# A pad of 192 bytes ahead of the weights' pool, so that all wide matmul operands begin at one address modulo 512

## The chip, the cores and the metric

The kernel runs on one core of a Trainium2 chip. The metric is the device time of one execution in microseconds. The engines that the text speaks of are TensorE (PE, the matmuls; PEld is its weight load), VectorE (DVE), ScalarE (ACT) and GpSimd (POOL); the SyncE queue (SP) issues the DMAs. A profile is one execution recorded by the hardware profiler.

## The reference

One block of a hybrid model for 512 tokens of width 1024, all in float32. A wide input projection feeds a state-space branch (SSD) and an attention branch with three dilations; both are gated and merged, and a gated feed-forward part with a short convolution follows.

```python
h = rms_norm(x, norm1_g[l])
proj = h @ w_in[l]
z, xbc, dt_raw, q, k, v, g_ssd, g_attn = jnp.split(proj, IN_SPLITS, axis=-1)
y_ssd = ssd_branch(z, xbc, dt_raw, ...)
y_attn = attn_branch(q, k, v, q_norm_g[l], k_norm_g[l])
merged = (jax.nn.sigmoid(g_ssd) * (y_ssd @ w_ssd_proj[l])
          + jax.nn.sigmoid(g_attn) * (y_attn @ w_attn_proj[l]))
x = x + merged @ w_out[l]
h2 = rms_norm(x, norm2_g[l])
u = causal_dwconv(h2 @ w_up[l], ffn_conv_w[l], ffn_conv_b[l])
u_gate, u_val = jnp.split(u, 2, axis=-1)
x = x + (jax.nn.silu(u_gate) * u_val) @ w_down[l]
```

## The kernel before

**How a product is made.** Every large product is done in split precision. A float32 operand is held as two tiles of the type float32r: a rounded part (`hh`, `h2h`, `mh`, `acth`, `whi` and so on) and the rest (`hl`, `h2l`, `ml`, `actl`, `wlo`). A product is the sum of three matmuls: high with high, high with low, low with high. A matmul of the wide kind loads a block of 128 rows by 128 columns as weights (the stationary operand) and streams a block of 128 by 512 past it (the moving operand) into one PSUM bank of 512 float32 columns.

**Weights.** All weight matrices come in 194 pieces of 128 x 1024 elements, in a fixed order (`pieces`). `load_piece` has SP fetch a piece into a `raw` tile; `make_piece` lets ScalarE round it to `whi` (L99) and VectorE subtract to `wlo` (L100). `raw`, `whi` and `wlo` have three buffers each in the pool `weights`. `prefetch` and `next_piece` make pieces ahead of their use.

**Stages.** TensorE's order is written out by hand; the other engines follow a scheduler, with hand-written order in two places. The stages of wide matmuls, by PSUM tile: `ps_v` (L401) projects the tokens to the attention values; `ps_qk` (L477) to queries and keys; `ps_ssd` and `ps_gate` (`mm_chan`, L139) to the SSD channels and the gates; `ps_ap` (`mm_chan`, L139) is the attention's output projection; `ps_sp` (L918) that of SSD; `ps_wo` (L945) the projection of the merged branches; `ps_u` (`mm_chan`, L139) the up projection; `ps_wd` (L945) the down projection. In `ps_v`, `ps_wo` and `ps_wd` the activations are stationary and the weights move; in all others the weights are stationary. `mm_chan` runs 24 matmuls per bank (8 blocks of 128 channels times three products; 12 for `ps_ap`, which has 4 blocks). Small matmuls of the SSD and attention sides are put in between during the input projection. `ps_dt` (L309) is a narrow product of `hh` and `hl` with `wd2`, a tile of 64 columns per block.

**Where tiles lie.** Memory is 128 partitions wide; a tile takes the same bytes in each, and an address here means the byte in a partition. Pools are stacked from two ends. On the left stack, upward: `const` (`cp`), then `weights` (`wp`), then in turn `comb`, `hT` (`hh`, `hl`), `ssd_a`, later `merged` (`mh`, `ml`), `ysplit` (`yh`, `yl`), then `ffn` and `act` (`acth`, `actl`). On the right stack, downward from 229,344: `ssd_y` (`ysb`), `attn_out` (`ah`, `al`), `attn_a`, `attn_b`, `ssd_b`, `gates`, later `x1` (`x1`, `h2h`, `h2l`) and `norm2`. Tiles take multiples of 32 bytes. The pool `const` goes from 16,512 to 24,864; `weights` begins at 24,864, which is 48 x 512 + 288. All wide tiles are multiples of 512 bytes long.

| tiles | stack | first address | modulo 512 |
|---|---|---|---|
| `raw`, `whi`, `wlo` | left | 24,864 (raw), 37,152 (whi), 49,440 (wlo) | 288 |
| `hh`, `hl` | left | 72,480, 88,864 | 288 |
| `mh`, `ml` | left | 61,728, 78,112 | 288 |
| `yh`, `yl` | left | 94,496, 106,784 | 288 |
| `acth`, `actl` | left | 67,872, 112,928 | 288 |
| `ah`, `al` | right | 180,192, 188,384 | 480 |
| `h2h`, `h2l` | right | 196,576, 212,960 | 480 |
| `wd2` | left, in `const` | 22,432 | 416, and 160 for every second block |

Of the kernel before, what the change touches and what calls it, by code (L numbers as in the profile page):

```python
# [8 lines left out]
F32 = mybir.dt.float32  # L9
# [7 lines left out]
P = 128  # L17
# [21 lines left out]
def kernel(  # L39
# [14 lines left out]
    def pool(name, side="left", bufs=1):  # L54
        return tc.tile_pool(name=name, bufs=bufs, side=side, reuse_waits="tile")

    cp = ctx.enter_context(pool("const"))
# [118 lines left out]
    dtd = cp.tile([P, NT, 32], F32, tag="dtd", name="dtd")  # L176
    cdec = cp.tile([P, NT, 32], F32, tag="cdec", name="cdec")
    wd2 = cp.tile([P, KD, 64], F32R, tag="wd2", name="wd2")
    scr_a = dp.tile([32, S], F32, tag="scr_a", name="scr_a")
    scr_e = dp.tile([32, S], F32, tag="scr_e", name="scr_e")  # L180
    stat = dp.tile([S, 3, 16], F32, tag="stat", name="stat")
# [929 lines left out]
```

## Time and profile before

| | us |
|---|---|
| median of three runs | 1229.72 (1226.87 to 1229.96) |
| the profiled execution | 1228.72 |
| span of its trace, first to last instruction | 1227.0 |
| TensorE busy | 1217.5 |
| VectorE busy | 686.6 |
| ScalarE busy | 545.3 |

The mean granted clock of TensorE over the span is 0.997 of full speed. A busy time is the union of the records of an engine or a group. The records of successive matmuls overlap, because a matmul's record runs to the modelled end of its pipeline while the next one has already begun; the pace of TensorE is therefore read from the starts of its matmuls and not from the length of a record. The two slices of the profile's second part that show TensorE's clock and the DMA traffic:

```profile
PEclk9999989999999999999999999999999999999999
DMA  5445434322746444434235323342433333322330
```

Each digit is a fortieth of the span, in tenths: the clock is full nearly everywhere, and the DMA engines are busy a third to a half of the time.

### The profile page before, as it was taken

The numbers are of one execution on the slowest core, as the hardware profiler recorded it, in microseconds if no ns is written. First come the engines' busy times: TensorE is split into PE (matmuls) and PEld (weight loads), VectorE is DVE, ScalarE is ACT, GpSimd is POOL, SyncE is SP. The second block draws the span as 40 slices with busy tenths as digits, with TensorE's granted clock in tenths as the row PEclk, the third lists the DMA queues.
The fourth block names the chain that finished last, engine by engine and source line by source line (L and its number), as shares of the span: only waits on it lengthen the run. The fifth ranks groups of instructions, "written<-read, shape, count | busy, mean of one in ns | idle before, by whom it ended". The sixth has DMA issues, their size and how long they took to land.

```text
span 1227.0 us, 15111 instructions
## 1 busy us (share of the span) xinstructions
PE 1217.5 (99%) x5992; PEld 992.5 (81%) x5992; DVE 686.6 (56%) x908; ACT 545.3 (44%) x829; POOL 79.3 (6%) x57
## 2 busy tenths in 40 slices
PE   9999989999999999999999999999999999999998
PEld 7877767997888788888888888888888888888887
DVE  5233444447789986877645445555665565653322
ACT  4433555377746656455533424423544444341210
POOL 1011111100000102101111000000000000000000
PEclk9999989999999999999999999999999999999999
DMA  5445434322746444434235323342433333322330
GB/s 183 120 112 138 105 87 106 93 66 74 189 121 184 127 127 131 121 112 110 71 87 140 118 88 101 102 173 69 119 88 100 89 97 92 94 95 96 105 126 35
DMA packets 157625, 134.71 MB, mean 110 GB/s; under 512 B 12337, under 2 KB 125601, under 8 KB 156530
## 3 DMA queue, kind: packets, MB, share of 16 engines
q1 hardware_dynamic: 157553, 133.74, 37.8%
q8 instruction: 47, 0.77, 0.3%
q14 instruction: 25, 0.20, 0.1%
HBM read 131.12 MB, written 2.61 MB: 109 GB/s over the span
## 4 chain that ended last, share of the span: by engine, by line
PE 91%; DVE 3%; DMA 3%; ACT 1%; POOL 1%; issue 1%; SPq 0%; POOLq 0%; DVEq 0%; ACTq 0%
PE ps_u L139 20%; PE ps_ssd L139 19%; PE ps_wd L945 10%; PE ps_qk L477 8%; PE ps_gate L139 7%; PE ps_sp L918 7%; PE ps_v L401 6%; PE ps_wo L945 4%; PE ps_ap L139 2%; DMA hrb<-scr_q 1%; PE ps_y L763 1%; PE ps_pv L578 1%; PE ps_s L540 1%; PE ps_o L768 1%; PE ps_pt L567 1%; POOL hrv L510 1%
## 5 line engine op out<-in xcount | busy, mean ns | idle before, releaser
L100 DVE TENSOR_TENSOR wlo<-raw,whi 128x1024 fp32r<-128x1024 f32 x194 | 243.3, 1255 | 373.3 <-ACT whi L99 237.5
L99 ACT CAST whi<-raw 128x1024 fp32r<-128x1024 f32 x194 | 203.4, 1049 | 338.5 <-PE ps_wd L945 79.8
L139 PE MATMUL ps_ssd<-hl,whi 128*128 128x512 f32 x384 | 103.0, 397 | 0.0
L139 PE MATMUL ps_ssd<-hh,whi 128*128 128x512 f32 x384 | 98.4, 398 | 0.0
L139 PE MATMUL ps_ssd<-hh,wlo 128*128 128x512 f32 x384 | 95.3, 390 | 0.0
L139 PE MATMUL ps_u<-h2h,whi 128*128 128x512 f32 (+1 forms) x368 | 90.0, 386 | 0.3 <-ACT h2h L214 0.2
L139 PE MATMUL ps_u<-h2l,whi 128*128 128x512 f32 (+1 forms) x368 | 89.5, 385 | 0.0
L139 PE MATMUL ps_u<-h2h,wlo 128*128 128x512 f32 (+1 forms) x368 | 89.5, 385 | 0.0
L139 PEld LDWEIGHTS ps_ssd<-hh,wlo 128*128 128x128 f32 x384 | 72.1, 188 | 15.8
L139 PEld LDWEIGHTS ps_ssd<-hh,whi 128*128 128x128 f32 x384 | 70.6, 188 | 14.0 <-issue 0.2
L139 PEld LDWEIGHTS ps_ssd<-hl,whi 128*128 128x128 f32 x384 | 70.2, 188 | 14.2 <-issue 0.5
L139 PEld LDWEIGHTS ps_u<-h2h,whi 128*128 128x128 f32 x368 | 67.2, 188 | 16.0 <-ACT h2h L214 0.8
L139 PEld LDWEIGHTS ps_u<-h2l,whi 128*128 128x128 f32 x368 | 67.1, 188 | 15.2
L139 PEld LDWEIGHTS ps_u<-h2h,wlo 128*128 128x128 f32 x368 | 67.1, 188 | 15.2
L52 DVE SCALAR_TENSOR_TENSOR facc<-ps_u,sc,facc 128x511 f32<-128x511 f32 x88 | 65.6, 746 | 5.7 <-ACT facc L1044 4.2
L477 PE MATMUL ps_qk<-hh,whi 128*128 128x512 f32 x192 | 62.6, 407 | 0.0
L477 PE MATMUL ps_qk<-hl,whi 128*128 128x512 f32 x192 | 60.2, 395 | 0.0
L477 PE MATMUL ps_qk<-hh,wlo 128*128 128x512 f32 x192 | 59.9, 393 | 0.0
L559 ACT ACTIVATE s<-s,st 128x128 f32<-128x128 f32 (+1 forms) x96 | 39.8, 417 | 33.8 <-DVE st L553 22.1
L945 PE MATMUL ps_wd<-whi,acth 128*128 128x512 f32 x176 | 54.2, 389 | 0.0
L945 PE MATMUL ps_wd<-whi,actl 128*128 128x512 f32 x176 | 54.2, 389 | 0.0
L945 PE MATMUL ps_wd<-wlo,acth 128*128 128x512 f32 x176 | 54.2, 389 | 0.0
(248 smaller groups left out, 1970.7 us busy)
## 6 DMA issues: line engine op xcount, KB each, us to landing
raw<-in_w_in_dram SPq DMA_DIRECT2D x100, 512.0 KB
raw<-in_w_up_dram SPq DMA_DIRECT2D x44, 512.0 KB
raw<-in_w_down_dram SPq DMA_DIRECT2D x22, 512.0 KB
bc<-scr_a SPq DMA_DIRECT2D x8, 1024.0 KB
raw<-in_w_ssd_proj_dram SPq DMA_DIRECT2D x16, 512.0 KB
hrb<-scr_q SPq DMA_DIRECT2D x12, 512.0 KB
eb<-scr_e SPq DMA_DIRECT2D x16, 256.0 KB
raw<-in_w_out_dram SPq DMA_DIRECT2D x8, 512.0 KB
```

The source lines that it names most:

```text
L52: nc.vector.scalar_tensor_tensor(o, a, s, b, op0=op0, op1=op1)
L99: nc.scalar.copy(hi, raw)
L100: nc.vector.tensor_sub(lo, raw, hi.bitcast(F32))
L139: nc.tensor.matmul(ps[:, t0:t0 + nt], a[:, k, c:c + n], b[:, k, t0:t0 + nt], start=(i == 0), stop=(i == total - 1))
L401: nc.tensor.matmul(pss[b], tok(g, kq * 2 + k, b, xx), w[:, k, :], start=(kq == 0 and j == 0 and k == 0), stop=(kq == 3 and j == 2 and k == 1))
L477: nc.tensor.matmul(pss[j], ww[:, k, j * P:(j + 1) * P], xx[:, kq * 2 + k, :], start=(kq == 0 and n == 0 and k == 0), stop=(kq == 3 and n = ...
L510: nc.gpsimd.tensor_tensor(rv, rv, nhalf.broadcast_to((P, 32)), op=ALU.pow)
L540: nc.tensor.matmul(pss[h][:, o:o + nk * P], qt[hp, j, q * P:(q + 1) * P], kt[hp, j, (q - nk + 1) * P:(q + 1) * P], start=True, stop=True)
L559: nc.scalar.activation(s[:, o:o + nk * P], s[:, o:o + nk * P], AF.Exp, bias=st[:, q, 0, 2 * j + h:2 * j + h + 1], accum_out=st[:, q, 1, 2 ...
L567: nc.tensor.transpose(pst[:, o:o + P], ss[h][:, o:o + P], ident)
L918: nc.tensor.matmul(pss[j], w[:, k, cs], ys[k][xi], start=(k2 == 0 and i == 0 and k == 0), stop=(k2 == 7 and i == 2 and k == 1))
L945: nc.tensor.matmul(pss[b], xx[:, k0 + k, b * P:(b + 1) * P], ww[:, k, :], start=(k0 == 0 and j == 0 and k == 0), stop=(k0 == nk - 2 and j ...
```

## The change

One tile more is taken from the pool `const`, 48 float32 numbers (192 bytes) in each partition. Nothing writes or reads it. It lies behind `wd2`, ahead of the small tiles of the pool that are made later; the pool's end, and with it the whole left stack above, moves up by 192 bytes. The right stack, which grows down from the other end, stays where it is. 288 + 192 = 480, so the wide tiles of both stacks begin at 480 modulo 512.

```diff
@@ -176,6 +176,8 @@
     dtd = cp.tile([P, NT, 32], F32, tag="dtd", name="dtd")
     cdec = cp.tile([P, NT, 32], F32, tag="cdec", name="cdec")
     wd2 = cp.tile([P, KD, 64], F32R, tag="wd2", name="wd2")
+
+    cp.tile([P, 48], F32, tag="pad", name="pad")
     scr_a = dp.tile([32, S], F32, tag="scr_a", name="scr_a")
     scr_e = dp.tile([32, S], F32, tag="scr_e", name="scr_e")
     stat = dp.tile([S, 3, 16], F32, tag="stat", name="stat")
```

## The prediction

> **What bounds the kernel now.** I read the engine shares first, then the chain that ended last, then the wide matmuls stage by stage.
>
> ```profile
> span 1227.0 us, 15111 instructions
> PE 1217.5 (99%) x5992; PEld 992.5 (81%) x5992; DVE 686.6 (56%) x908; ACT 545.3 (44%) x829; POOL 79.3 (6%) x57
> PE 91%; DVE 3%; DMA 3%; ACT 1%; POOL 1%; issue 1%; SPq 0%; POOLq 0%; DVEq 0%; ACTq 0%
> ```
>
> TensorE holds 91% of the chain, and in the long stages it never stops. So the time is a count of matmuls times the distance from one matmul's start to the next. A busy share can't show that distance, because each matmul's record runs on while the next has started; it has to be worked out from starts. The next rows are those of the groups by shape (count, busy us, mean ns of one).
>
> ```profile
> L139 PE MATMUL ps_u<-h2l,whi 128*128 128x512 f32 x336 | 85.2, 396 | 0.0
> L139 PE MATMUL ps_u<-h2h,wlo 128*128 128x512 f32 x336 | 85.2, 396 | 0.0
> L139 PE MATMUL ps_u<-h2h,whi 128*128 128x512 f32 x336 | 85.2, 395 | 0.0
> L945 PE MATMUL ps_wd<-whi,acth 128*128 128x512 f32 x176 | 54.2, 389 | 0.0
> L139 PE MATMUL ps_ap<-ah,whi 128*128 128x512 f32 x32 | 8.8, 394 | 0.0
> ```
>
> The same instruction, 128 rows by 128 columns of weights against 512 moving columns, records 389 ns in one stage and 394 to 396 in two others. Now the timeline of TensorE (start, length, line, operands, count), at four places where the wide matmuls run with nothing else between them.
>
> ```profile
> 644.99 2.00 PE L139 MATMUL ps_gate<-hh,whi 128*128 128x512 f32 x8
> 646.83 1.98 PE L139 MATMUL ps_gate<-hl,whi 128*128 128x512 f32 x8
> ...
> 661.33 0.84 PE L139 MATMUL ps_gate<-hh,whi 128*128 128x512 f32 x3
> ...
> 699.41 1.09 PE L139 MATMUL ps_ap<-ah,whi 128*128 128x512 f32 x4
> ...
> 721.81 0.62 PE L918 MATMUL ps_sp<-yh,whi 128*128 128x512 f32 x2
> ...
> 868.29 2.02 PE L139 MATMUL ps_u<-h2h,whi 128*128 128x512 f32 x8
> ...
> 1103.49 0.63 PE L945 MATMUL ps_wd<-whi,acth 128*128 128x512 f32 x2
> ```
>
> And the rows of two tiles, with the first and last start of each group:
>
> ```profile
> L945 PE MATMUL ps_wd<-wlo,acth x176: 388/389/389, 1104.4 to 1223.0; 128*128 128x512 f32 x176
> L945 PE MATMUL ps_wo<-whi,mh x64: 389/389/477, 808.9 to 852.2; 128*128 128x512 f32 x64
> ```
>
> Start to start:
> - gate: nine groups of 8 lie between 644.99 and 661.33, so 16.34 us / 72 = 226.9 ns.
> - ssd projection (`ps_sp`): 8 weight pieces x 4 banks x 6 matmuls x 2 halves = 384 between 721.81 and the first `ps_wo` at 808.9, so 87.1 / 384 = 226.8 ns.
> - down projection (`ps_wd`): 528 matmuls, the first at 1103.49, the last at 1223.0, so 119.5 / 527 = 226.8 ns.
> - up projection (`ps_u`), 3 x 336 = 1008 wide ones between 868.29 and 1103.49: 235.20 / 1008 = **233.3 ns**.
> - attention projection (`ps_ap`), 96 between 699.41 and 721.81: 22.40 / 96 = **233.3 ns**.
>
> What sets the two slow stages apart is neither the loop (gate, up and attention projection all come from L139) nor the engine's clock, as this table of stretches shows (up, attention projection, gate, down; length, busy us of each engine, granted clock, DMA share, GB/s):
>
> ```profile
> 868.30:1103.40 235.10, 235.10 (x1010) 189.46 (x1009) 140.42 (x169) 103.66 (x129) 0.00 (x0) 1.00 0.33 97
> 699.40:721.70 22.30, 22.30 (x97) 17.88 (x96) 12.98 (x17) 7.47 (x11) 0.00 (x0) 1.00 0.28 94
> 645.00:695.00 50.00, 50.00 (x222) 41.40 (x221) 22.39 (x26) 15.78 (x20) 4.35 (x4) 1.00 0.49 137
> 1103.50:1223.00 119.50, 119.50 (x529) 98.90 (x527) 31.93 (x31) 21.45 (x21) 0.00 (x0) 1.00 0.27 91
> ```
>
> The clock is 1.00 in all four, and the gate stage, at 226.9, has more DMA traffic than either slow one. It is the addresses. These are from the allocation of the kernel before, not from the profile: everything on the left stack that is wide (`whi`, `wlo`, `hh`, `hl`, `yh`, `yl`, `mh`, `ml`, `acth`, `actl`) begins at 288 modulo 512; the right stack (`ah`, `al`, `h2h`, `h2l`) at 480. Every step inside these tiles from one matmul to the next is a multiple of 512 bytes, except the strided tokens of `ps_v`. So the five stages that take both operands from the left have equal residues, and exactly the two that read right-hand data against left-hand weights are 192 apart and 6.5 ns slower. A sixth case stands in the timeline: `ps_dt` reads `hh` at 288 against `wd2` at 416 or 160, with only 64 columns of weights.
>
> ```profile
> 76.84 2.00 PE L309 MATMUL ps_dt<-hh,wd 128*64 128x512 f32 x8
> 78.68 1.99 PE L309 MATMUL ps_dt<-hl,wd 128*64 128x512 f32 x8
> 80.51 0.63 PE L477 MATMUL ps_qk<-hh,whi 128*128 128x512 f32 x2
> ```
>
> (80.51 - 76.84) / 16 = 229.4 ns: the moving tile that runs at 226.9 against `whi` costs 2.5 more here, with half the weights to load and residues 128 apart. That speaks for the distance between the two operands rather than for where one of them lies.
>
> **The change part by part.** It adds one tile of 192 bytes per partition and no instruction, no DMA, no wait. The left stack above it moves by 192; 288 becomes 480. The right stack stays. No tile of one stack comes to overlap another pool's tile that it didn't overlap before: the gaps at the meeting points are larger than 192 bytes (the nearest, `bct` below `kt1`, is 544 bytes and becomes 352).
>
> - Up projection: 1008 x (233.3 - 226.8) = 1008 x 6.5 = **-6.6 us**. All of it lies on the path: TensorE idles nowhere between 868.3 and 1103.4 (235.10 busy of 235.10).
> - Attention projection: 96 x 6.5 = **-0.6 us**, on the path too (22.30 of 22.30).
> - The 96 up matmuls of 256 columns are shorter and partly wait for the norm. Half as much to gain per matmul would be 96 x 3.3 = 0.3 us; I take 0, bounds -0.3 to 0.
> - Stages with both operands on the left (`ps_v` 288, `ps_qk` 576, `ps_ssd` 1152, `ps_gate` 384, `ps_sp` 384, `ps_wo` 192, `ps_wd` 528: 3504 matmuls): both residues move together. I take 0. No row shows a matched pair at 480, so the bounds are 6.5 ns either way, 3504 x 6.5 = 22.8 us; the nearest row is `ps_dt` above, which puts the cost on the distance.
> - Small matmuls that mix a moved and an unmoved operand: `ps_o`, `ps_xt`, `ps_bt`, and `ps_dt`, whose distance goes from 128 to 64.
>
> ```profile
> L768 PE MATMUL ps_o<-bct,prev 128*128 128x128 f32 x96 | 15.0, 292 | 0.0
> L732 PE MATMUL ps_xt<-ident,xst 128*128 128x128 f32 x64 | 9.6, 272 | 0.0
> L719 PE MATMUL ps_bt<-ident,bct 128*128 128x128 f32 x24 | 3.9, 272 | 0.0
> ```
>
> They are mismatched before and after. At 6.5 ns each, 184 + 16 of them are 1.3 us; I take 0, bounds -1.3 to +1.3.
> - What would be late next, when the up projection asks for its weights sooner. A piece serves 24 matmuls, so it is wanted every 5.44 us instead of 5.60. These waits of the stretch 854 to 1104 (total us, times, longest) show the preparation waiting for TensorE to free a buffer, not the other way:
>
> ```profile
> DVE wlo L100 <- PE ps_u L139: 75.1, 40, 2.9
> ACT whi L99 <- PE ps_u L139: 6.1, 21, 0.5
> ```
>
> VectorE waits 75.1 / 40 = 1.9 us for a buffer before each `wlo`; the 0.16 us that a piece loses comes out of that. If the cover were gone, at most 44 pieces x 0.16 = 7 us would return. DMA moves 97 GB/s here and would move 100, less than the 137 of the gate stage above. Price: 0. DVE, ACT and DMA meet the same new residues, but their operations lie under that slack.
>
> Sum: -6.6 - 0.6 = **-7.2 us**. The profiled execution took 1228.72 us with its span of 1227.0 (1.7 around it), so it becomes 1221.5; against the median of 1229.72 it is 1222.5. I say 1222.0.
>
> The Trainium skill bears on the step that everything hangs on. TensorE: Matmul & The Clock Gate, § Step-by-step: what each phase is for, holds that the stationary and the moving operand come through two independent SBUF read ports, and that "Loading the next tile's weights doesn't steal SBUF read bandwidth from the running matmul." By that rule no distance between two addresses would matter and the sum would be 0. The trace differs as far as it goes: 226.8 against 233.3 ns for one shape, one loop and one granted clock, split exactly as the residues are.
>
> **The rivals.**
> 1. *Nothing happens.* What sets the two slow stages apart could be that the moving operand lies in the upper part of memory, above 180,000 bytes, and not its residue; or the pad could be dropped, or not move the pool. Then 1008 and 96 matmuls stay at 233.3, and the time stays at about 1229. For it: the two slow stages do share that place as well as the residue. Against it: `ps_dt` is slowed with its moving operand low in memory. That the weights' load never disturbs the running matmul, as the skill's sentence has it, ends here too.
> 2. *Slower: residue 480 itself is what costs.* In the two slow stages the moving operand lies at 480, so distance and place can't be parted by them. If the place were the cause, the 3504 matched matmuls would go to 233.3 as well and the two slow stages would stay: +3504 x 6.5 = +22.8 us, about 1252. It decides as soon as a matched pair at 480 costs more than 226.8 by 7.2 / (3504 + 1104) = 1.6 ns. Against it stands `ps_dt` again: slowed with its moving operand at 288.
> 3. *Only part of it.* The distance matters, but 480 against 480 doesn't reach 226.8; half the gain gives 1225.6.
> 4. *More than forecast.* A matched pair at 480 is better than one at 288. Taking 1 ns as the size, 3504 ns more go: 1218.5. No row speaks for it.
>
> **How the numbers follow.** The forecast gets 0.80, rival 1 gets 0.07, rival 2 gets 0.04, rival 3 gets 0.06, rival 4 gets 0.03. A measurement of this kernel can tell about 0.3%, 3.7 us, from no change. Faster by more than that: the forecast, rival 4 and rather more than half of rival 3, 0.87; within: rival 1 and the rest of rival 3, 0.09; slower: 0.04. The forecast's own range comes from the spread of the runs before (1226.87 to 1229.96, less 7.2: 1219.7 to 1222.8) and the small terms (-1.6 to +1.3): 1218.1 to 1224.1. To reach 8 in 10 it takes in half a gain as well, so 1218 to 1225.6.
>
> **What would show it.** In the profile after: `ps_u` wide, 8 matmuls in 1.81 us instead of 1.87, and a mean record of 389 ns, not 396; `ps_ap` groups of 4 every 0.91 us instead of 0.93; `ps_gate`, `ps_sp` and `ps_wd` unchanged at 226.8; `ps_wd` beginning some 7 us earlier, and all of the difference lying in the two stages. The prediction is wrong if `ps_u` keeps 233.3, if the matched stages leave 226.8, or if VectorE's wait for `ps_u` vanishes and TensorE shows idle time there.

## The result, and the profile after

| | before | after |
|---|---|---|
| median | 1229.84 us (1226.87 to 1230.35) | 1221.65 us (1219.76 to 1222.36) |
| ratio | | 0.9936, interval 0.9916 to 0.9956 |
| span of the profiled execution | 1227.0 us | 1219.3 us |

The medians are of four runs each. The change makes the kernel 0.64% faster, 8.2 us between the medians; the interval of the ratio is 5.4 to 10.3 us. The prediction was -7.2 us and 1222.0.

The profile after, its engine line and, from the groups by shape, the two stages that were slow and one that wasn't (count, busy us, mean ns of one record):

```profile
PE 1209.0 (99%) x5992; PEld 991.0 (81%) x5992; DVE 687.5 (56%) x908; ACT 545.2 (45%) x829; POOL 77.2 (6%) x57
```

```profile
L139 PE MATMUL ps_u<-h2h,whi 128*128 128x512 f32 x336 | 83.0, 389 | 0.0
L947 PE MATMUL ps_wd<-whi,acth 128*128 128x512 f32 x176 | 54.2, 389 | 0.0
L139 PE MATMUL ps_ap<-ah,whi 128*128 128x512 f32 x32 | 8.6, 389 | 0.0
```

All three now record 389 ns; the up projection had 395 to 396 and the attention projection 394. The instructions are as many as before, and the busy time of VectorE and ScalarE is within 1 us of what it was; TensorE gave up 8.5 us of busy time. The same places of its timeline as in the prediction (start, length, line, operands, count):

```profile
698.59 1.07 PE L139 MATMUL ps_ap<-ah,whi 128*128 128x512 f32 x4
...
720.35 0.61 PE L920 MATMUL ps_sp<-yh,whi 128*128 128x512 f32 x2
...
867.32 2.00 PE L139 MATMUL ps_u<-h2h,whi 128*128 128x512 f32 x8
...
1095.82 0.62 PE L947 MATMUL ps_wd<-whi,acth 128*128 128x512 f32 x2
```

And the first start of two groups, in the rows of their tiles:

```profile
L947 PE MATMUL ps_wo<-whi,mh x64: 389/389/476, 807.4 to 850.7; 128*128 128x512 f32 x64
L139 PE MATMUL ps_u<-h2h,whi x368: 277/389/397, 853.3 to 1092.0; 128*128 128x512 f32 x168, 128*128 128x256 f32 x16
```

Taking each stretch from the first start of one stage to the first start of the next, the two spans differ in this way:

| stretch | before, us | after, us | difference |
|---|---|---|---|
| up to the attention projection | 699.41 | 698.59 | -0.8 |
| attention projection, 96 wide | 22.40 | 21.76 | -0.6 |
| ssd projection, 384 wide | 87.1 | 87.05 | 0 |
| merged projection, with transposes | 45.9 | 45.9 | 0 |
| up projection, 256 columns, with transposes | 13.5 | 14.0 | +0.5 |
| up projection, 1008 wide | 235.20 | 228.50 | -6.7 |
| down projection and the end | 123.5 | 123.5 | 0 |
| span (the rows add up to it but for rounding) | 1227.0 | 1219.3 | -7.7 |

The up projection now runs at 228.50 / 1008 = 226.7 ns and the attention projection at 21.76 / 96 = 226.7 ns. The 0.8 us ahead of the attention projection isn't explained by the change: in three other kernels of this study in which the attention and the up projection run at 226.7 ns (right stack moved, 256 alone, `wd2` matched), that stretch ends between 697.2 and 699.7. Of the 0.8 us, 0.5 lie ahead of the first `ps_qk` matmul, which starts at 36.82 us before and at 36.29 after; in those three it starts between 36.2 and 36.8.

### The profile page after: what moved, and what is told of

Read it like the earlier page. It is cut to its first block, busy times and chain, and to the rows that moved or that the text cites. A ratio compares the mean times of both kernels' runs of the same rounds, so it can differ in the third digit from the quotient of the medians.

```text
span 1219.3 us, 15111 instructions
## 1 busy us (share of the span) xinstructions
PE 1209.0 (99%) x5992; PEld 991.0 (81%) x5992; DVE 687.5 (56%) x908; ACT 545.2 (45%) x829; POOL 77.2 (6%) x57
## 4 chain that ended last, share of the span: by engine, by line
PE 93%; DMA 2%; DVE 1%; POOL 1%; ACT 1%; issue 0%; SPq 0%; POOLq 0%; ACTq 0%; DVEq 0%
PE ps_ssd L139 22%; PE ps_u L139 20%; PE ps_wd L947 10%; PE ps_qk L479 8%; PE ps_gate L139 7%; PE ps_sp L920 7%; PE ps_v L403 5%; PE ps_wo L947 3%; PE ps_ap L139 2%; DMA hrb<-scr_q 1%; PE ps_y L765 1%; PE ps_o L770 1%; PE ps_pv L580 1%; PE ps_s L542 1%; POOL hrv L512 1%; PE ps_pt L569 1%
```

## The experiments

The theory: the pace of a wide matmul depends on the distance between the addresses of the moving operand and of the weights. The rivals: the moving operand costs by its place (high in memory), or it was the weights' new place that helped. Below, a distance is moving minus weights. The paces in the text are mean distances from start to start, inside one stage, with gaps above 300 ns left out, where other matmuls come in.

**The other stack moved instead.** A pad at the top of the right stack, and none in the left.

```diff
+    rp = ctx.enter_context(pool("right_pad", side="right"))
+    rp.tile([P, 48], F32, tag="rpad", name="rpad")
     yp_cm = pool("ssd_y", side="right")
```

> The left stack stays at 288 modulo 512; a permanent pad of 192 bytes at the top of the right stack brings ah, al, h2h and h2l to 288 as well. Distance theory (what costs is the distance modulo 512 between the moving operand and the weights): up and attention projection run at 226.8 ns start to start, all other stages unchanged, 7 to 8 us faster than the kernel before, about 1222. Place theory (moving operands high in memory cost, and in the changed kernel it was the weights' new place that helped): up and attention projection stay at 233.3, about 1229.

1221.14 us, ratio 0.9929 (0.9911 to 0.9947). The timeline of its up projection:

```profile
902.18 1.98 PE L139 MATMUL ps_u<-h2h,wlo 128*128 128x512 f32 x8
904.00 1.98 PE L139 MATMUL ps_u<-h2h,whi 128*128 128x512 f32 x8
...
909.44 1.98 PE L139 MATMUL ps_u<-h2h,whi 128*128 128x512 f32 x8
```

Three groups of 8 between 904.00 and 909.44 are 226.7 ns each. The weights lie where they lay before and `h2h` is still high in memory, and the gain is whole. Both forms of the place rival fall.

**Both stacks moved**, the pad of the change and that of the last kernel together: left 480, right 288.

> Both pads: the left stack at 480, the right stack at 288, so moving minus weights is -192 (320 modulo 512) in the up and attention projections and 0 in the others. Distance theory: the matched stages stay at 226.8 ns; up and attention projection are again above 226.8, by up to 7 ns if 320 costs what 192 does (about 1229), less if it doesn't. Place theory (weights at 480 are what helps): up and attention projection at 226.8, about 1222.

1223.99 us, ratio 0.9955 (0.9939 to 0.9971). The matched stages keep 226.7 to 226.9 ns. The up projection runs at 228.9 and the attention projection at 229.1: above 226.7, but far from 233.3. Two rows of the up projection:

```profile
901.13 2.00 PE L139 MATMUL ps_u<-h2h,whi 128*128 128x512 f32 x8
...
906.62 2.00 PE L139 MATMUL ps_u<-h2h,whi 128*128 128x512 f32 x8
```

24 matmuls in 5.49 us are 228.8 ns. A distance of 320 costs 2.2 ns where 192 costs 6.6, so the price of a distance has to be measured.

**Only the up projection put back to 192**, at other addresses than before: the change, and 320 bytes behind `h2l`, which puts `h2h` and `h2l` at 160 against weights at 480.

```diff
     h2l = x1p.tile([P, KD, S], F32R, tag="h2l", name="h2l")
+    x1p.tile([P, 80], F32, tag="pad_h2l", name="pad_h2l")
```

> The left stack and ah, al at 480 as in the changed kernel; h2h and h2l pushed to 160, so that the up projection alone has the distance 192 again, at other places than in the kernel before. Distance theory: up projection back at 233.3 ns, every other stage at 226.8, some 6.6 us slower than the changed kernel. Place theory: up projection stays at 226.8.

1228.43 us, one run (the kernel before, on the same chip, had a median of 1229.47). The up projection:

```profile
901.57 2.03 PE L139 MATMUL ps_u<-h2h,whi 128*128 128x512 f32 x8
...
907.17 2.03 PE L139 MATMUL ps_u<-h2h,whi 128*128 128x512 f32 x8
```

24 matmuls in 5.60 us are 233.3 ns, with both operands at addresses that the kernel before doesn't have; the attention projection stays at 226.7. The cost goes with the distance.

**The mismatch everywhere.** 192 bytes ahead of `hh`, 320 ahead of `mh`, 384 ahead of `yh`, 320 ahead of `act_h`, so that nearly every wide matmul has the distance 192.

```diff
+    hT.tile([P, 48], F32, tag="pad_hh", name="pad_hh")
...
+    mp.tile([P, 80], F32, tag="pad_mh", name="pad_mh")
...
+        sp.tile([P, 96], F32, tag="pad_yh", name="pad_yh")
...
+            late["act"].tile([P, 80], F32, tag="pad_acth", name="pad_acth")
```

> The mismatch of the kernel before put everywhere: hh, hl, yh, yl at 480 and mh, ml, acth, actl at 96 against weights at 288, so each wide matmul but ps_v's strided ones has the distance 192. Distance theory: gate, ssd projection, merged and down projection at about 233 ns instead of 226.8; with some 3200 matmuls at 6.5 ns that is 15 to 21 us slower than the kernel before, 1245 to 1251. If the two slow stages were slow for another reason, about 1229.

1245.02 us, one run. Gate, SSD channels, attention, ssd, merged, up and down projection all run between 233.3 and 233.4 ns. The gate stage, for one, in its timeline:

```profile
658.22 2.03 PE L139 MATMUL ps_gate<-hh,whi 128*128 128x512 f32 x8
...
663.82 2.03 PE L139 MATMUL ps_gate<-hh,whi 128*128 128x512 f32 x8
```

24 matmuls in 5.60 us again, in a stage that has 226.9 in the kernel before. Placement alone is thus worth some 1245.0 - 1221.65 = 23 us in this kernel, with not one instruction changed.

**Many distances at once.** Each operand gets a distance of its own, by pads ahead of or behind the tiles (in bytes: `hh` 32, `hl` 32, `mh` 64, `ml` 64, `yh` 32, `yl` 64, `acth` 32, `actl` 64; behind `ah` 32, `al` 64, `h2h` 64, `h2l` 384).

> Weights at 288; each operand that meets them gets a distance of its own (moving minus weights, modulo 512): hh 32, hl 64, ah 96, al 128, yh 160, yl 224, h2h 256, h2l 320, and where the weights move: mh 448, ml 384, acth 480, actl 416. Distance theory: each group runs at a pace of its own between 226.7 and some 234 ns, also where both operands are low in memory; a pace below 226.7 would mean that distance 0 isn't the best. Place theory: only ah, al, h2h and h2l are above 226.8.

1237.95 us, one run. The place rival fails here too: `yh` and `yl`, low in memory, run at 233.3. But the row that matters is the up projection, with `h2h` at 256 and `h2l` at 320:

```profile
950.55 1.98 PE L139 MATMUL ps_u<-h2h,whi 128*128 128x512 f32 x8
952.36 2.01 PE L139 MATMUL ps_u<-h2l,whi 128*128 128x512 f32 x8
954.21 1.99 PE L139 MATMUL ps_u<-h2h,wlo 128*128 128x512 f32 x8
956.03 1.98 PE L139 MATMUL ps_u<-h2h,whi 128*128 128x512 f32 x8
```

The groups on `h2h` with `whi` take 1.81 us and those on `h2l` 1.85; over the stage that is 226.8 and 230.9 ns each. The groups on `h2h` with `wlo`, which follow those on `h2l`, take 1.82 to 1.83, 228.3 each. A distance of 256 thus looks as good as 0.

**256 alone.** The pad of the change with 448 bytes instead of 192.

```diff
-    cp.tile([P, 48], F32, tag="pad", name="pad")
+    cp.tile([P, 112], F32, tag="pad", name="pad")
```

> The pad of the change is 448 bytes instead of 192: the left stack at 224 modulo 512, the right one at 480, so the operands of the up and attention projections are 256 apart and all others 0. If only residues modulo 512 count, the two stages stay above 226.8 ns (233 ns and about 1229 if 256 costs what 192 does). If residues modulo 256 count, as the high half of scan1 suggests, the two stages run at 226.7 and the time is that of the changed kernel, about 1221.5.

1222.23 us, ratio 0.9949 (0.9933 to 0.9965), the changed kernel's time within the intervals. The up projection:

```profile
901.14 1.98 PE L139 MATMUL ps_u<-h2h,whi 128*128 128x512 f32 x8
...
906.59 1.98 PE L139 MATMUL ps_u<-h2h,whi 128*128 128x512 f32 x8
```

5.45 us for 24, 227 ns; over the stage it is 226.7. The equality has to hold modulo 256 only; the 512 of the change's description is more than is needed.

**The other distances**, the same for the high and the low operand of a stage, in three kernels.

> Weights at 288; one distance for the high and the low operand of a stage: up 128, gate and SSD channels 64, attention projection 32, ssd projection 96, and with weights moving: merged projection 480, down projection 416. Distance modulo 256: every stage lies above 226.7, between 228 and 234 ns, and none below 226.7. If only the one distance of 192 were bad, up would be at 226.8 here.

> The same with the distances changed round: up 64, gate and SSD channels 128, attention projection 160, ssd projection 32, merged projection 352, down projection 480. If the distance alone sets the pace, up at 64 runs like gate at 64 in scan2 (within 1 ns) and gate at 128 like up at 128 there. If the stage matters (which side the weights are on, other traffic), the pairs differ.

In the third, the wide operands are slices of tiles that are 256 bytes longer, so that a distance can be finer than 32 bytes:

```diff
+    def shifted(pool, nk, o, name):
+        t = pool.tile([P, nk * S + 64], F32R, tag=name, name=name)
+        return t[:, o:o + nk * S].rearrange("p (k s) -> p k s", k=nk)
...
-    h2h = x1p.tile([P, KD, S], F32R, tag="h2h", name="h2h")
+    h2h = shifted(x1p, KD, 20, "h2h")
```

> Distances finer than the 32 bytes of a tile's place, by starting inside a longer tile (moving minus weights, modulo 256): gate and SSD channels 8, up 16, attention projection -4, ssd projection -16, and with weights moving: merged projection -8, down projection -4. If only exact equality modulo 256 is free, every stage is above 226.7 ns. If the two reads meet in lines or banks of some bytes, the smallest distances still run at 226.7. A pace below 226.7 would make a version that beats the changed kernel.

They take 1242.91, 1241.86 and 1241.73 us (one run each). The pace by distance modulo 256 (480, 416 and 352 are 224, 160 and 96; -4, -8 and -16 are 252, 248 and 240), of matmuls with 128 columns of weights and 512 moving columns:

| distance | pace, ns (stage) |
|---|---|
| 0 | 226.7 (every clean stage; residues 288, 480, and 224 against 480) |
| 8 | 233.3 (gate) |
| 16 | 231.7 (up) |
| 32 | 233.4 (attention), 233.3 (ssd projection) |
| 64 | 228.9 (up), 229.1 (attention), 228.9 and then 233.3 (gate) |
| 96 | 233.3 (ssd projection), 233.4 (merged) |
| 128 | 232.4 (up), 233.0 (gate) |
| 160 | 234.2 (attention), 234.3 (down) |
| 192 | 233.3 (all) |
| 224 | 233.3 (merged, down) |
| 240 | 236.6 (ssd projection) |
| 248 | 230.7 (merged) |
| 252 | 230.2 (attention), 232.4 (down) |

Only the equality is free, down to a distance of 4 bytes, and nothing is below it, so these runs point to no better distance for the stages of the table than the changed kernel has. One part of the wide matmuls isn't at this pace in any kernel: 192 of the 288 of `ps_v` take every fourth token as weights, a strided read, and run at 235.4 ns before and after the change. No run here lays those tokens out in another way, so what they could gain is open.

One expectation failed: at 64, gate and up differ by up to 4.4 ns, though their distance is one (at 128 they agree within 1 ns). At 252 the attention and the down projection differ by 2.2 ns as well, and no run here shows why. For 64 the timeline of the gate stage in the first of the three kernels shows where the difference arises:

```profile
640.96 2.00 PE L139 MATMUL ps_gate<-hl,whi 128*128 128x512 f32 x8
...
648.28 2.00 PE L139 MATMUL ps_gate<-hh,wlo 128*128 128x512 f32 x8
650.12 0.39 PE L785 MATMUL ps_n<-sr,ones_r 128*1 128x512 f32 x1
650.35 0.40 PE L786 MATMUL ps_n<-sr,ones_r 128*1 128x512 f32 x1
650.58 2.03 PE L139 MATMUL ps_gate<-hh,whi 128*128 128x512 f32 x8
...
661.78 2.03 PE L139 MATMUL ps_gate<-hh,whi 128*128 128x512 f32 x8
```

Up to 648.28, 32 matmuls take 7.32 us, 228.8 each; after two small matmuls with one column of weights, 48 take 11.20 us, 233.3 each, and the stage keeps that pace until it ends. One distance has two steady paces, and what comes in between goes with which: the pair of small matmuls is followed directly by wide matmuls of the SSD channels or the gates four times in this kernel, and each time they run at 233.3; behind other small matmuls they come back to 228.9. At 0 a stage falls back to 226.7 within some ten matmuls after such a disturbance, in the kernel before as in the changed one.

**Also `wd2` matched**: the pad split, 64 bytes ahead of `wd2` and 128 behind it.

```diff
+    cp.tile([P, 16], F32, tag="pad0", name="pad0")
     wd2 = cp.tile([P, KD, 64], F32R, tag="wd2", name="wd2")
-    cp.tile([P, 48], F32, tag="pad", name="pad")
+    cp.tile([P, 32], F32, tag="pad", name="pad")
```

> The changed kernel with its pad of 192 bytes split, 64 ahead of wd2 and 128 behind it, so that wd2 has the residue of hh modulo 256 as well. Distance theory: ps_dt, with weights of 64 columns, falls from 228.5 ns (distance 64 in the changed kernel; 229.3 at 128 in the kernel before) to 226.7; everything else as in the changed kernel, the time the same within its spread. If what remains above 512 columns at full clock were the weights' load, half of it should run below 226.7.

1221.62 us, one run, the changed kernel's time. But `ps_dt` doesn't do what the theory says:

```profile
76.79 2.01 PE L312 MATMUL ps_dt<-hh,wd 128*64 128x512 f32 x8
78.64 2.00 PE L312 MATMUL ps_dt<-hl,wd 128*64 128x512 f32 x8
80.47 0.62 PE L480 MATMUL ps_qk<-hh,whi 128*128 128x512 f32 x2
```

3.68 / 16 = 230.0 ns at distance 0, against 229.4 at 128 in the kernel before. By the 15 intervals inside the product it is 229.9 at 0, 229.3 at 128 and, in the changed kernel, 228.5 at 64. The product is short, but its intervals repeat: at 0 the same six come round (236, 229, 224, 227, 234, 230), and they do so again in the second of the three kernels above, where `hh` and `wd2` happen to be at distance 0 too. For weights of 64 columns, equal residues aren't the best case.

## Why the prediction was right

- **The sum.** The span fell by 7.7 us where 7.2 were forecast. The two terms gave 7.3; the 256-column matmuls took 0.5 back, and 0.8 came from the early stretch, which the change doesn't explain. That the last two nearly cancel, and the median came within 0.4 us of 1222.0, is luck; the 7.3 are not.
- **What bounds the kernel, and the two slow stages.** Right. The time was a count of matmuls times a pace, and the two stages with right-hand operands took the pace of the others: 226.7 ns, where 226.8 was forecast.
- **The up projection, -6.6 us**: -6.7. **The attention projection, -0.6 us**: -0.6.
- **The 3504 matched matmuls, 0**: the ssd and down projections run at 226.7 as before. A matched pair at 480 is as good as at 288, and in the kernel with 256 so are residues of 224 against 480. The prediction speaks of five stages with equal residues where its own list has seven, and it had shown the pace of three. It also counts all of `ps_v` as matched; the 192 matmuls with strided tokens run at 235.4 ns before and after, so their 0 held although they were never at the fast pace.
- **The 96 matmuls of 256 columns, -0.3 to 0.** Wrong in sign. These are rows of the timeline of the kernel before and of the changed one:

```profile
863.76 1.07 PE L139 MATMUL ps_u<-h2h,wlo 128*128 128x256 f32 x8
...
867.38 1.07 PE L139 MATMUL ps_u<-h2l,whi 128*128 128x256 f32 x8
```

```profile
862.52 1.12 PE L139 MATMUL ps_u<-h2h,wlo 128*128 128x256 f32 x8
...
866.36 1.12 PE L139 MATMUL ps_u<-h2l,whi 128*128 128x256 f32 x8
```

Four groups take 3.62 us before, 113 ns each, and 3.84 us after, 120 ns each. The stretch became 0.5 us longer, where half the gain of a wide matmul was assumed from the wide rows. In the kernel with the mismatch everywhere it is 113.3 again. In the one with only the up projection put back to 192, the last 48 of the 96 settle at 113.3, the two 24s ahead of them at 117.8: here too one distance has two paces. The distance that costs 6.6 ns at 512 columns gives the best pace seen at 256.
- **The small mixed matmuls, 0 within 1.3 us**: right as far as it can be seen. The intervals of `ps_o`, `ps_xt` and `ps_bt` stay within 0.3 ns of what they were (132.0, 109.2 and 109.3 before; 132.0, 109.0 and 109.1 after), and `ps_dt` goes from 229.3 to 228.5.
- **The weights' preparation, 0.** Right: TensorE has no idle time in the wide up projection (229.00 busy of 229.00 between 866.7 and 1095.7), and VectorE's wait for a buffer there fell from 75.1 us to this row:

```profile
DVE wlo L100 <- PE ps_u L139: 65.9, 39, 2.8
```

That is 9.2 us over 44 pieces, 0.2 us each, about the 0.16 that a piece lost.
- **`ps_dt` as the evidence for the distance.** This step failed as an argument, though its conclusion held; as far as the chances rested on it, that was luck. Its 229.4 ns at distance 128 were read as the cost of a mismatch, and rivals 1 and 2 were given small chances on that ground. At distance 0 it runs at 230.0. So it couldn't tell distance from place; the kernel with the right stack moved and the one with the up projection put back do.
- **"Modulo 512".** The prediction took it over from the residues in the table; modulo 256 is what counts.

The prediction weighed a rule of the Trainium skill (TensorE: Matmul & The Clock Gate, § Step-by-step: what each phase is for): the weights' load doesn't take read bandwidth from the running matmul. The times of this kernel don't bear it out: 226.7 against 233.3 ns for one instruction stream at two distances.

That the distance between the two operands sets the pace is shown. That their two reads of one memory get in each other's way is an inference from it; no run here shows the reads themselves. Why 64 and 252 cost less than 8 and 240 stays open, as does what makes two steady paces at 64.

## What to carry to other kernels

Where TensorE runs without idle time, compare the start-to-start pace of one matmul shape between stages; a difference without a waiting engine can come from addresses, and a pad that costs nothing can take it away. For weights of 128 columns against 512 moving columns in this number type, the runs here say that both operands should begin at the same address modulo 256; the blocks inside the tiles lie at multiples of 512 in all of them. For the two other shapes seen here the best distance is another one, so for a new shape it has to be measured; a row of one shape is no evidence for another.

## What was not expected of the hardware

- The best pace per column is the same for both shapes: 226.7 / 512 = 0.443 ns with a distance of 0, and 113.3 / 256 = 0.443 ns with a distance of 192. No steady stretch of these two shapes in the runs here is below it. The Trainium skill (TensorE: Matmul & The Clock Gate, § Back-to-back issue gap) has a formula for the isolated gap of one matmul at full clock, by which 512 columns take an estimated 512 / 2.4 + 2.5 = 216 ns. No stage here shows that.
- One distance can have two steady paces (228.8 and 233.3 ns at 64 with 512 columns; 117.8 and 113.3 at 192 with 256), and two small matmuls in between are enough to go from one to the other at 64.
- A distance of 4 or 8 bytes already costs 3.5 to 6.6 ns per matmul.
